# The modulation vector with output channels on partitions: one fused VectorE operation per weight tile

## The chip, the cores and the metric

The kernel runs as one program on one core of a Trainium2 chip. The metric is the device time of one execution in microseconds. Besides TensorE (PE) the core has VectorE (DVE), ScalarE (ACT), GpSimd (POOL) and the sync engine (SP), which issues most DMAs; each takes its instructions in its own order, and semaphores tie them together.

## The reference

Two transformer blocks of width 2048 work on 256 tokens, all in fp32. The first block is modulated by a conditioning vector `c` of 2048 numbers; that modulation is the part that changes:

```python
cond = jax.nn.silu(c)                                   # (1, 2048)
mod = cond @ w_ada[i] + b_ada[i]                        # (2048) x (2048, 12288)
shift1, scale1, gate1, shift2, scale2, gate2 = jnp.split(mod, 6, axis=-1)
h = _rms(x, norm1_w) * (1 + scale1) + shift1            # then in_proj, SSM, attention
x = x + gate1 * mixed
h2 = _rms(x, norm2_w) * (1 + scale2) + shift2           # then the gated FFN
x = x + gate2 * ffn
```

Everything else (projections, a state-space mixer, dilated attention, a second block with neighbourhood, latent and memory attention and a second FFN) is matrix products with 256 rows and small work between them.

## The kernel before, in words

Every weight comes in tiles of 1 MB (128 partitions by 2048 floats) through a ring of six buffers `r`; SP issues the loads in the order of one list `W`. A tile of a matrix product is split into two fp32r parts, halves of 1024 columns at a time: ACT copies it to `h` (line 207) and DVE computes the rest `l = r - h` (line 208). TensorE then makes three products per tile (lines 221, 222 and 226, the last of them on `l`).

The 96 tiles of `w_ada` (kind "a" in the list) are strewn between those (function `mixed`): 32 tiles for shift1 and scale1 among the first products, 48 for gate1, shift2 and scale2 among the next, 16 for gate2 in the first FFN. They don't go to TensorE. A tile holds 2 x 128 input channels by 1024 output channels, input channels on partitions, and the generator `s_ada` gives it to DVE: two operations (line 950) `acc += r[:, j] * cond[j]`, with `cond` one number per partition. Eight tiles make one half of one of the six vectors (1024 outputs), whose sum over partitions still has to be taken. `ada_end` does that on TensorE: for shift and scale eight products with a column of ones (line 969, each in two passes, so 16 matmul records), which put output channels on partitions, and a small DVE operation (973 or 975) that fetches them; for a gate two products of 512 columns with a matrix of ones (line 960), which spread the row over all partitions, and two ACT copies (962). `acc` has two buffers; POOL clears one (945) and ACT loads the bias into its first row (946).

The order on every engine is the order in which the Python generators emit: `Flow.run` goes through the list, hands an "a" tile to `s_ada`, splits a "w" tile, sends the tile before it to the products, and then lets every waiting task take one step. No scheduler changes it later.

Of the kernel before, what the change touches and what calls it, by code (L numbers as in the profile page):

```python
# [10 lines left out]
F32 = mybir.dt.float32  # L11
F32R = mybir.dt.float32r
AF = mybir.ActivationFunctionType
OP = mybir.AluOpType
# [9 lines left out]
SP = 4  # L24
# [20 lines left out]


def _vec_layout():
    names = (("c", 16), ("norm1_w", 16), ("norm2_w", 16), ("mem_norm_2", 16),
             ("ln_mix_2", 16), ("ln_mem_2", 16), ("ln_ffn_2", 16), ("q_norm_w", 1),
             ("k_norm_w", 1), ("q_norm_2", 4), ("kv_norm_2", 2), ("na_out_norm_2", 8),  # L50
             ("mla_out_norm_2", 8))
    out, o = {}, 0
    for n, k in names:
        out[n] = (o, k)
        o += k
    return out, o
# [28 lines left out]
def layout(inp):  # L85
    g = {k: np.asarray(v) for k, v in inp.items()}
    perm = _token_order()
    a = {}
    a["x"] = np.ascontiguousarray(g["x"][0][perm].reshape(2, 128, 4, 512).transpose(2, 1, 0, 3))
    a["mem"] = np.ascontiguousarray(g["mem_2"][0].reshape(2, 128, 4, 512).transpose(2, 1, 0, 3))  # L90
    a["vec"] = np.concatenate([_pp(g[n].reshape(-1)) for n in VEC], axis=1)
    a["b_ada"] = np.ascontiguousarray(g["b_ada"].reshape(1, 12288))
    a["fnorm"] = np.ascontiguousarray(g["final_norm_2"].reshape(1, 2048))
    a["bias1"], a["rope"] = _constants()
    a["w_ada"] = np.ascontiguousarray(
        g["w_ada"][0].reshape(8, 2, 128, 12, 1024).transpose(3, 0, 2, 1, 4))
    a["w_in"] = _wtiles(g["w_in"][0])
    a["w_glu"] = _wtiles(g["ssm_w_glu"][0])
    a["w_out"] = _wtiles(g["w_out"][0])
    for s, d in (("w_ffn_gate", "wg1"), ("w_ffn_up", "wu1"), ("w_ffn_down", "wd1"),  # L100
                 ("w_gate_2", "wg2"), ("w_up_2", "wu2"), ("w_down_2", "wd2"),
                 ("w_out_2", "w_out2"), ("w_xq_2", "w_xq"), ("w_xk_2", "w_xk"),
                 ("w_xv_2", "w_xv"), ("w_xo_2", "w_xo")):
        a[d] = _wtiles(g[s][0])
    w2 = g["w_in_2"][0]
    a["w_qkv2"] = _wtiles(np.ascontiguousarray(w2[:, :3072]))
    a["w_cq"] = _wtiles(np.ascontiguousarray(w2[:, 3072:3584]))
    a["w_ckv"] = _wtiles(np.ascontiguousarray(w2[:, 3584:]), 320)
    uq = g["w_uq_2"][0].reshape(512, 8, 192)
    a["w_uq"] = _wtiles(np.concatenate([uq[:, :, :128].reshape(512, 1024),  # L110
                                        uq[:, :, 128:].reshape(512, 512)], axis=1))
    kv = g["w_ukv_2"][0].reshape(256, 8, 2, 128).transpose(0, 2, 1, 3).reshape(2, 128, 2, 2, 512)
    a["w_ukv"] = np.ascontiguousarray(kv.transpose(2, 1, 3, 0, 4)).reshape(2, 1, 128, 4, 512)
    rpb = g["na_rpb_2"][0]
    t = perm.reshape(2, 128)
    r, c = t // 64, t % 64
    rk, ck = perm // 64, perm % 64
    start = np.clip(c - 8, 0, 48)
    ok = (ck[None, None] >= start[..., None]) & (ck[None, None] < start[..., None] + 16)
    dr = rk[None, None] - r[..., None] + 7  # L120
    dc = np.clip(ck[None, None] - c[..., None] + 15, 0, 30)
    nb = np.where(ok[None], rpb[:, dr, dc], np.float32(-1e30))
    a["nabias"] = np.ascontiguousarray(nb.transpose(0, 2, 1, 3).reshape(8, 128, 512))

    def state(v):
        return v.reshape(32, 2, 64).transpose(1, 2, 0).reshape(128, 32)

    ldt = np.repeat(g["ssm_log_dt"][0].reshape(64, 1), 64, axis=1)
    dd = np.tile(g["ssm_d"][0].reshape(32, 32).T, (4, 1))
    a["ssm_p"] = np.ascontiguousarray(  # L130
        np.stack([state(g["ssm_a_re"][0]), state(g["ssm_a_im"][0]), state(ldt), dd], 1))
    bc = []
    for i, n in enumerate(("ssm_b_re", "ssm_b_im", "ssm_c_re", "ssm_c_im")):
        v = g[n][0]
        if i >= 2:
            v = v.transpose(0, 2, 1)
        bc.append(v.reshape(NSEC, SP, 2, 64, 16).transpose(0, 2, 3, 1, 4).reshape(NSEC, 128, SP, 16))
    a["ssm_bc"] = np.ascontiguousarray(np.stack(bc, 2))
    return a
# [299 lines left out]
class Ssm:  # L439
# [272 lines left out]
    def run(self, s, u4, ytok):  # L712

        k, nc = self.k, self.k.nc
        V, G = nc.vector, nc.gpsimd
        xt, C, T, E = self.sec.pop(s)
        unit = lambda: k.unit((128, 2, SP, 64))
        S = k.pm((128, 2, SP, 64))
# [4 lines left out]
        a, b, c = unit(), unit(), unit()  # L723
# [19 lines left out]
                nc.tensor.matmul(ps[:, q, 1:64], C[:, i, q, 1:5].rearrange("p a b -> p (a b)"),  # L743
                                 a[:, i, q, 0:63], start=False, stop=i == 1)
        self.done = s
        y4 = self.pool.tile([128, SP, 64], F32, name=k.nm("y"), tag="y4", bufs=2)
        nc.scalar.activation(y4, ps, AF.Gelu_apprx_tanh)
        yield
        for h in range(2):
# [6 lines left out]
def build(ctx, tc, A, out):  # L756
# [20 lines left out]
    def v(n, i, m=1):  # L777
        return vec[:, VEC[n][0] + i:VEC[n][0] + i + m]
# [110 lines left out]
            x[g][t] = unit()  # L889
            S.dma_start(x[g][t], A["x"][g][:, t])  # L890

    cond = k.const([128, 16], "cond")
    S.activation(cond, v("c", 0, 16), AF.Silu)
    wqk = k.const([128, 1], "wqk")
    V.tensor_tensor(wqk, v("q_norm_w", 0), v("k_norm_w", 0), op=OP.mult)
    V.tensor_scalar(wqk, wqk, 128.0 ** -0.5, None, op0=OP.mult)
# [38 lines left out]
        return done  # L935


    md = {i: k.const([128, 16], f"mod{i}") for i in (0, 1, 3, 4)}
    gate = {2: [], 5: []}

    def s_ada():

        for h in (2, 0, 3, 1) + ADA + (10, 11):
            acc = k.up.tile([128, 1024], F32, name=k.nm("acc"), tag="acc", bufs=2)
            G.memset(acc, 0.0)
            S.dma_start(acc[0:1], A["b_ada"][:, h * 1024:h * 1024 + 1024])
            for kb in range(8):
                r = yield
                for j in range(2):
                    V.scalar_tensor_tensor(acc, r[:, j], cond[:, 2 * kb + j:2 * kb + j + 1], acc,  # L950
                                           op0=OP.mult, op1=OP.add)
            fl.add(ada_end(h // 2, h % 2, acc))
        yield

    def ada_end(i, half, acc):
        if i in gate:
            yield
            for j in range(2):
                ps = k.pm()
                PE.matmul(ps, k.ones, acc[:, 512 * j:512 * j + 512], start=True, stop=True)  # L960
                row = (unit if i == 2 else unit2)()
                S.activation(row, ps, AF.Copy)
                gate[i].append(row)
            return
        yield
        yield
        ps = k.pm((128, 8))
        for j in range(8):
            PE.matmul(ps[:, j:j + 1], acc[:, j * 128:(j + 1) * 128], k.ones[:, 0:1], start=True, stop=True)
        o = md[i][:, 8 * half:8 * half + 8]  # L970
        if i in (1, 4):
            w = v("norm1_w" if i == 1 else "norm2_w", 8 * half, 8)
            V.scalar_tensor_tensor(o, ps, 1.0, w, op0=OP.add, op1=OP.mult)
        else:
            V.tensor_copy(o, ps)
        got.add((i, half))
        yield

# [660 lines left out]
```

## Time and profile before

| | |
|---|---|
| time, median of 3 runs | 2726.45 us (2726.13 to 2727.95) |
| the profiled execution | 2723.84 us, of it the span from first to last instruction 2721.8 us |
| TensorE busy | 2628.7 us (97% of the span) |
| VectorE busy | 1691.5 us (62%) |
| ScalarE busy | 1258.8 us (46%) |
| GpSimd busy | 103.2 us (4%) |
| DMA | 577.97 MB, mean 212 GB/s |
| DVE line 950 (the modulation) | 192 operations, 245.8 us, from 31.0 to 862.6 us |

A busy TensorE is not one at its peak, since its matmuls overlap and their ends are modelled; so stretches are compared by what waits for what. The work of the modulation lies in the first 884 us only. From 884 to 2650 us nothing of it is left.

### The profile page before, as it was taken

How to read it: one execution, taken by the hardware profiler on the slowest of the kernel's cores; microseconds unless marked ns; L12 is line 12 of the kernel's file. 1: busy time of each engine (PE TensorE's matmuls, PEld its weight loads, DVE VectorE, ACT ScalarE, POOL GpSimd, SP SyncE). 2: the span in 40 equal slices, each digit the busy share in tenths (PEclk: the TensorE clock that was granted, in tenths of full speed). 3: DMA queues.
4: the chain of work that ended last, by engine and by line, in shares of the span. 5: the costliest groups of instructions: out<-in, count | busy, mean ns of one | idle time of the engine just before them, and what ended most of it. 6: DMA issues, size and time to landing. Idle time of an engine off the chain costs nothing.

```text
span 2721.8 us, 31521 instructions
## 1 busy us (share of the span) xinstructions
PE 2628.7 (97%) x12272; PEld 2184.9 (80%) x12272; DVE 1691.5 (62%) x2128; ACT 1258.8 (46%) x1786; POOL 103.2 (4%) x115
## 2 busy tenths in 40 slices
PE   8989988988999999999999999999999999999998
PEld 6778777776788888888888878888888888888887
DVE  7996999979676554555465454655554544455444
ACT  5464545553544444433445555554544433443433
POOL 3000000100000000000000021100000000000001
PEclk9999999999999999999999999999999999999999
DMA  8988766667576555555545434455455555555552
GB/s 337 346 302 321 278 239 227 239 228 305 221 284 267 190 185 198 187 199 186 194 164 191 178 132 147 178 189 183 170 213 194 191 191 191 196 186 185 186 200 94
DMA packets 90029, 577.97 MB, mean 212 GB/s; under 512 B 9996, under 2 KB 12428, under 8 KB 22680
## 3 DMA queue, kind: packets, MB, share of 16 engines
q1 hardware_dynamic: 80928, 561.61, 55.5%
q10 hardware_dynamic: 8952, 14.34, 1.6%
q8 instruction: 96, 1.57, 0.2%
q14 instruction: 53, 0.43, 0.0%
HBM read 569.63 MB, written 6.29 MB: 212 GB/s over the span
## 4 chain that ended last, share of the span: by engine, by line
PE 79%; DVE 11%; issue 7%; ACT 2%; DMA 1%; POOL 0%; SPq 0%; ACTq 0%; DVEq 0%; POOLq 0%
PE g L226 25%; PE g L221 24%; PE g L222 24%; DVE l L208 3%; DVE acc L950 2%; PE m L238 2%; DVE v L627 1%; ACT h L207 0%; PE m L342 0%; DVE u L732 0%; PE m L1488 0%; PE m L1475 0%; DVE C L635 0%; PE m L240 0%; PE m L329 0%
## 5 line engine op out<-in xcount | busy, mean ns | idle before, releaser
L208 DVE TENSOR_TENSOR l<-r,h 128x1024 fp32r<-128x1024 f32 x866 | 1028.2, 1222 | 562.5 <-ACT h L207 554.9
L221 PE MATMUL g<-h,u 128*128 128x512 f32 x3424 | 1353.0, 395 | 9.2 <-ACT h L207 6.2
L222 PE MATMUL g<-h,u 128*128 128x512 f32 x3424 | 1337.8, 391 | 0.0
L207 ACT ACTIVATE h<-r 128x1024 fp32r<-128x1024 f32 x866 | 884.6, 1056 | 634.7 <-PE g L222 596.6
L226 PE MATMUL g<-l,u 128*128 128x512 f32 x3424 | 922.1, 391 | 39.9 <-DVE l L208 39.7
L226 PEld LDWEIGHTS g<-l,u 128*128 128x128 f32 x3424 | 642.5, 189 | 185.2 <-DVE l L208 52.4
L221 PEld LDWEIGHTS g<-h,u 128*128 128x128 f32 x3424 | 648.0, 189 | 144.8 <-ACT h L207 10.3
L222 PEld LDWEIGHTS g<-h,u 128*128 128x128 f32 x3424 | 647.8, 189 | 132.3 <-issue 1.0
L950 DVE SCALAR_TENSOR_TENSOR acc<-r,cond,acc 128x1024 f32<-128x1024 f32 x192 | 245.8, 1280 | 3.8
L271 ACT ACTIVATE u<-m 128x512 fp32r<-128x512 f32 (+1 forms) x80 | 42.7, 574 | 163.8 <-PE m L238 128.8
L291 ACT ACTIVATE j<-u 128x512 bf16<-128x512 f32 (+2 forms) x92 | 47.3, 514 | 121.1 <-DVE u L1208 34.1
L272 DVE TENSOR_TENSOR u<-m,u 128x512 fp32r<-128x512 f32 (+1 forms) x80 | 50.0, 658 | 85.5 <-ACT u L271 85.4
L274 ACT ACTIVATE u<-m,vec 128x256 fp32r<-128x256 f32 x86 | 38.8, 471 | 74.7 <-PE m L342 32.4
L238 PE MATMUL m<-ident,u 128*128 128x128 f32 x372 | 53.0, 286 | 16.8 <-DMA u<-in_mem_dram 7.8
L275 DVE SCALAR_TENSOR_TENSOR u<-m,vec,u 128x256 fp32r<-128x256 f32 x86 | 40.0, 481 | 45.9 <-ACT u L274 45.9
L238 PEld LDWEIGHTS m<-ident,u 128*128 128x128 f32 x372 | 45.6, 147 | 24.2 <-ACT u L982 6.8
L1255 DVE TENSOR_TENSOR w<-g,w 128x512 f32<-128x512 f32 x24 | 16.5, 687 | 43.4 <-PE g L226 43.4
L1239 DVE SCALAR_TENSOR_TENSOR w<-g,r,w 128x512 f32<-128x512 f32 x22 | 15.5, 747 | 44.4 <-PE g L226 44.4
L299 POOL TENSOR_TENSOR r<-s,mhalf 128x2 f32<-128x2 f32 x5 | 4.4, 889 | 1010.1 <-DVE s L298 1010.1
L1237 DVE TENSOR_TENSOR w<-g,w 128x512 f32<-128x512 f32 x22 | 14.2, 685 | 44.3 <-PE g L226 44.3
L1511 DVE TENSOR_TENSOR u<-g,u 128x512 f32<-128x512 f32 x22 | 14.2, 685 | 44.3 <-PE g L226 44.3
L1231 ACT ACTIVATE w<-g,r 128x512 f32<-128x512 f32 x22 | 13.9, 686 | 52.9 <-PE g L226 52.9
(237 smaller groups left out, 1221.3 us busy)
## 6 DMA issues: line engine op xcount, KB each, us to landing
r<-in_w_ada_dram SPq DMA_DIRECT2D x96, 1024.0 KB, 5.1
r<-in_wg_dram SPq DMA_DIRECT2D x88, 1024.0 KB, 4.8
r<-in_wu_dram SPq DMA_DIRECT2D x88, 1024.0 KB, 4.8
r<-in_wd_dram SPq DMA_DIRECT2D x88, 1024.0 KB, 4.8
r<-in_w_in_dram SPq DMA_DIRECT2D x32, 1024.0 KB, 5.8
r<-in_w_out_dram SPq DMA_DIRECT2D x32, 1024.0 KB, 5.2
r<-in_w_qkv_dram SPq DMA_DIRECT2D x24, 1024.0 KB, 4.8
r<-in_w_xk_dram SPq DMA_DIRECT2D x16, 1024.0 KB, 9.1
```

Of the source, the lines that this page charges most:

```text
L207: nc.scalar.activation(h, r, AF.Copy)
L208: (nc.gpsimd if shared else nc.vector).tensor_tensor(l, r, h.bitcast(F32), op=OP.subtract)
L221: nc.tensor.matmul(ps[t][:, :n], al[:, s], h[:, k], start=first and k == 0, stop=False)
L222: nc.tensor.matmul(ps[t][:, :n], ah[:, s], h[:, k], start=False, stop=False)
L226: nc.tensor.matmul(ps[t][:, :n], ah[:, s], l[:, k], start=False, stop=last and k == len(acts) - 1)
L238: self.nc.tensor.transpose(o, i, self.ident)
L271: nc.scalar.activation(h, ps, AF.Copy)
L272: nc.vector.tensor_tensor(l, ps, h.bitcast(F32), op=OP.subtract)
L274: nc.scalar.activation(h, ps, AF.Copy, scale=w)
L275: nc.vector.scalar_tensor_tensor(l, ps, w, h.bitcast(F32), op0=OP.mult, op1=OP.subtract)
L291: self.nc.scalar.activation(j[:, :n], src, AF.Square, accum_out=acc)
L950: V.scalar_tensor_tensor(acc, r[:, j], cond[:, 2 * kb + j:2 * kb + j + 1], acc, op0=OP.mult, op1=OP.add)
```

## The change

`w_ada` is laid out the other way round: a tile holds 128 output channels (on partitions) by all 2048 input channels (along the row). `cond` becomes a full tile of 128 x 2048, the same row in every partition, loaded by a broadcasting DMA of 1 MB and put through Silu by ACT. One `tensor_tensor_reduce` per tile multiplies the tile by `cond` (writing the product back into the tile) and gives the row sum, started from the bias, as one column of `md`. The bias comes with the other small vectors. Shift and scale need no TensorE product any more. A gate, wanted as a row on all partitions, is built from its column: four ACT copies of the identity, scaled by the column, make a block-diagonal tile `d` of 128 x 512, and the product with ones spreads it. `acc`, its clearing and its bias loads are gone. For room, the tile `y4` of the state-space mixer has one buffer instead of two, and a scratch size for dynamic DMA is set.

```diff
@@ _vec_layout, layout
-    names = (("c", 16), ("norm1_w", 16), ...
+    names = (("norm1_w", 16), ...
-             ("mla_out_norm_2", 8))
+             ("mla_out_norm_2", 8), ("b_ada", 96))
-    a["b_ada"] = np.ascontiguousarray(g["b_ada"].reshape(1, 12288))
+    a["c"] = np.ascontiguousarray(g["c"].reshape(1, 2048))
     a["w_ada"] = np.ascontiguousarray(
-        g["w_ada"][0].reshape(8, 2, 128, 12, 1024).transpose(3, 0, 2, 1, 4))
+        g["w_ada"][0].reshape(2048, 12, 8, 128).transpose(1, 2, 3, 0))
@@ Ssm.run
-        y4 = self.pool.tile([128, SP, 64], F32, name=k.nm("y"), tag="y4", bufs=2)
+        y4 = self.pool.tile([128, SP, 64], F32, name=k.nm("y"), tag="y4", bufs=1)
@@ build
-    cond = k.const([128, 16], "cond")
-    S.activation(cond, v("c", 0, 16), AF.Silu)
+    cond = k.const([128, 2048], "cond")
+    S.dma_start(cond, A["c"].to_broadcast([128, 2048]))
+    S.activation(cond, cond, AF.Silu)
@@ s_ada, ada_end
-    md = {i: k.const([128, 16], f"mod{i}") for i in (0, 1, 3, 4)}
+    md = {i: k.const([128, 16], f"mod{i}") for i in range(6)}
         for h in (2, 0, 3, 1) + ADA + (10, 11):
-            acc = k.up.tile([128, 1024], F32, name=k.nm("acc"), tag="acc", bufs=2)
-            G.memset(acc, 0.0)
-            S.dma_start(acc[0:1], A["b_ada"][:, h * 1024:h * 1024 + 1024])
-            for kb in range(8):
+            for j in range(8):
                 r = yield
-                for j in range(2):
-                    V.scalar_tensor_tensor(acc, r[:, j], cond[:, 2 * kb + j:2 * kb + j + 1], acc,
-                                           op0=OP.mult, op1=OP.add)
-            fl.add(ada_end(h // 2, h % 2, acc))
+                n = 8 * (h % 2) + j
+                V.tensor_tensor_reduce(r, r, cond, 1.0, v("b_ada", 8 * h + j), OP.mult, OP.add,
+                                       md[h // 2][:, n:n + 1])
+            fl.add(ada_end(h // 2, h % 2))
         if i in gate:
             yield
             for j in range(2):
+                d = (unit if i == 2 else unit2)((128, 4, 128))
+                for c in R4:
+                    n = 8 * half + 4 * j + c
+                    S.activation(d[:, c], k.ident, AF.Copy, scale=md[i][:, n:n + 1])
                 ps = k.pm()
-                PE.matmul(ps, k.ones, acc[:, 512 * j:512 * j + 512], start=True, stop=True)
+                PE.matmul(ps, k.ones, d.rearrange("p a b -> p (a b)"), start=True, stop=True)
                 row = (unit if i == 2 else unit2)()
                 S.activation(row, ps, AF.Copy)
                 gate[i].append(row)
             return
         yield
-        yield
-        ps = k.pm((128, 8))
-        for j in range(8):
-            PE.matmul(ps[:, j:j + 1], acc[:, j * 128:(j + 1) * 128], k.ones[:, 0:1], start=True, stop=True)
-        o = md[i][:, 8 * half:8 * half + 8]
         if i in (1, 4):
-            w = v("norm1_w" if i == 1 else "norm2_w", 8 * half, 8)
-            V.scalar_tensor_tensor(o, ps, 1.0, w, op0=OP.add, op1=OP.mult)
-        else:
-            V.tensor_copy(o, ps)
+            o = md[i][:, 8 * half:8 * half + 8]
+            V.scalar_tensor_tensor(o, o, 1.0, v("norm1_w" if i == 1 else "norm2_w", 8 * half, 8),
+                                   op0=OP.add, op1=OP.mult)
         got.add((i, half))
@@ kernel
-    nc = bacc.Bacc("TRN2", target_bir_lowering=False, num_devices=1)
+    nc = bacc.Bacc("TRN2", target_bir_lowering=False, num_devices=1, dynamic_dma_scratch_size=512)
```

On DVE, around the first tile of the modulation, the order before is this (`r` is the tile, `l` and `h` the parts of a weight tile, `u` and `m` belong to the memory activations):

```order
L275 SCALAR_TENSOR_TENSOR u_347<-m_341,vec,u_346 128x256 x2
L275 SCALAR_TENSOR_TENSOR u_358<-m_352,vec,u_357 128x256 x2
L950 SCALAR_TENSOR_TENSOR acc_180<-r_155,cond,acc_180 128x1024 x2
L208 TENSOR_TENSOR l_370<-r_183,h_369 128x1024
L208 TENSOR_TENSOR l_374<-r_183,h_373 128x1024
```

And this is the same place in the changed kernel:

```order
L275 SCALAR_TENSOR_TENSOR u_347<-m_341,vec,u_346 128x256 x2
L275 SCALAR_TENSOR_TENSOR u_358<-m_352,vec,u_357 128x256 x2
L948 ISA r_158,mod_112<-r_158,cond,vec 128x2048
L948 ISA mod_112 128x1
L208 TENSOR_TENSOR l_369<-r_183,h_368 128x1024
L208 TENSOR_TENSOR l_373<-r_183,h_372 128x1024
```

Nothing moved: in place of two operations of 1024 columns stand one of 2048 columns and a second, one-column instruction that writes the sum to `mod`.

On ACT, at the first half of gate2 in the first FFN, the order before (`w` are tiles of the second pool, `m` is a PSUM tile, `h` the first part of a weight tile):

```order
L207 ACTIVATE h_6553<-r_6438 128x1024
L207 ACTIVATE h_6557<-r_6438 128x1024
L962 ACTIVATE w_6590<-m_6588 128x512
L962 ACTIVATE w_6594<-m_6592 128x512
L207 ACTIVATE h_6604<-r_6476 128x1024
L207 ACTIVATE h_6608<-r_6476 128x1024
```

And in the changed kernel, where line 964 is the copy of a finished row and `mod_116` the column of gate2:

```order
L207 ACTIVATE h_6376<-r_6266 128x1024
L207 ACTIVATE h_6380<-r_6266 128x1024
L960 ACTIVATE w_6411<-ident,mod_116 128x128 x4
L964 ACTIVATE w_6418<-m_6416 128x512
L960 ACTIVATE w_6420<-ident,mod_116 128x128 x4
L964 ACTIVATE w_6427<-m_6425 128x512
L207 ACTIVATE h_6436<-r_6303 128x1024
L207 ACTIVATE h_6440<-r_6303 128x1024
```

The second block-diagonal tile stands behind the copy of the first row, which waits for TensorE's first product; before, TensorE's two products stood side by side with nothing of ACT between them.

## Rows read from the trace of the kernel before

**Rows 1.** The page's first part: busy us, share of the span, instructions.
```profile
PE 2628.7 (97%) x12272; PEld 2184.9 (80%) x12272; DVE 1691.5 (62%) x2128; ACT 1258.8 (46%) x1786; POOL 103.2 (4%) x115
```
**Rows 2.** Windows: length, busy us of PE, PEld, DVE, ACT, POOL; PEclk, DMA share, GB/s.
```profile
5.00:10.00 5.00, 1.99 (x8) 1.54 (x8) 1.84 (x4) 1.78 (x4) 4.92 (x5) 1.00 0.97 357
30.00:204.00 174.00, 157.10 (x724) 126.67 (x723) 165.33 (x290) 90.25 (x140) 10.18 (x10) 0.97 0.88 321
204.00:272.00 68.00, 67.26 (x320) 56.00 (x319) 47.23 (x45) 30.87 (x40) 1.91 (x2) 1.00 0.81 321
272.00:544.00 272.00, 244.89 (x1324) 207.56 (x1323) 260.20 (x484) 139.46 (x294) 16.38 (x14) 0.96 0.65 246
544.00:680.00 136.00, 114.53 (x527) 92.24 (x526) 116.63 (x146) 62.89 (x102) 1.59 (x2) 0.96 0.70 266
748.00:884.00 136.00, 136.00 (x606) 111.45 (x605) 90.80 (x81) 56.55 (x64) 0.00 (x0) 1.00 0.72 275
```
**Rows 3.** Windows of line 950 alone: length, busy us of DVE, PEclk, DMA.
```profile
30.00:204.00 174.00, 63.98 (x50) 0.97 0.88 321
272.00:544.00 272.00, 84.37 (x66) 0.96 0.65 246
544.00:680.00 136.00, 38.38 (x30) 0.96 0.70 266
```
**Rows 4.** DVE groups: line, shapes, count | busy us, mean ns | idle before, releaser.
```profile
L208 DVE TENSOR_TENSOR l<-r,h 128x1024 fp32r<-128x1024 f32 x858 | 1022.1, 1226 | 560.2 <-ACT h L207 554.5 <-DMA r<-in_w_qkv_dram 1.9
L1256 DVE TENSOR_TENSOR u<-u,w 128x512 f32<-128x512 f32 x24 | 16.6, 692 | 0.8
L975 DVE COPY mod<-m 128x8 f32<-128x8 f32 x4 | 0.7, 164 | 6.0 <-PE m L969 5.9
```
**Rows 5.** DVE timeline, 88 to 102 us: start, duration, engine, line, operation, count.
```profile
88.63 2.35 DVE L208 TENSOR_TENSOR l<-r,h 128x1024 fp32r<-128x1024 f32 x2
...
91.33 0.18 DVE L468 TENSOR_TENSOR s<-pr,pi 128x32 f32<-128x32 f32 x1
91.43 0.18 DVE L468 TENSOR_TENSOR s<-pi,pr 128x32 f32<-128x32 f32 x1
...
99.20 2.60 DVE L950 SCALAR_TENSOR_TENSOR acc<-r,cond,acc 128x1024 f32<-128x1024 f32 x2
101.71 1.22 DVE L208 TENSOR_TENSOR l<-r,h 128x1024 fp32r<-128x1024 f32 x1
```
**Rows 6.** ACT timeline, 0 to 14 us; brackets: idle before, releaser.
```profile
2.90 0.22 ACT L893 ACTIVATE cond<-vec 128x16 f32<-128x16 f32 x1 [0.45 <-DMA vec<-in_vec_dram]
...
11.01 2.00 ACT L207 ACTIVATE h<-r 128x1024 fp32r<-128x1024 f32 x2 [1.76 <-DMA u<-in_mem_dram]
...
13.44 0.19 ACT L291 ACTIVATION_READ_ACCUMULATOR j<-u 128x1 f32 x1
13.66 0.63 ACT L291 ACTIVATE j<-u 128x512 bf16<-128x512 f32 x1
```
**Rows 7.** PE timeline, 210 to 213 us, at a half of shift and scale.
```profile
210.83 1.84 PE L969 MATMUL m<-ones,acc 128*128 128x1 f32 x16
212.53 0.49 PE L221 MATMUL g<-h,u 128*128 128x512 f32 x1
```
**Rows 8.** Timeline of PE and ACT at gate2 (784 us), and ACT at 365 us.
```profile
784.29 1.88 PE L960 MATMUL m<-acc,ones 128*128 128x512 f32 x4
785.35 0.60 ACT L962 ACTIVATE w<-m 128x512 f32<-128x512 f32 x1 [6.14 <-PE m L960]
...
365.53 2.45 ACT L1066 ACTIVATE u<-u,s 128x128 f32<-128x128 f32 x8
```
**Rows 9.** Timeline of ACT and DVE at the mixer's second `y4`, 334 to 346 us.
```profile
334.60 0.38 ACT L747 ACTIVATE y<-m 128x256 f32<-128x256 f32 x1 [1.98 <-PE m L743]
...
338.27 0.50 DVE L750 STREAM_TRANSPOSE u<-y 128x128 f32<-128x128 f32 x2
...
343.82 2.35 DVE L208 TENSOR_TENSOR l<-r,h 128x1024 fp32r<-128x1024 f32 x2
```

More of the change, by code (lines that the diff above doesn't have):

```diff
@@ L47, in _vec_layout @@
 def _vec_layout():
-    names = (("c", 16), ("norm1_w", 16), ("norm2_w", 16), ("mem_norm_2", 16),
+    names = (("norm1_w", 16), ("norm2_w", 16), ("mem_norm_2", 16),
              ("ln_mix_2", 16), ("ln_mem_2", 16), ("ln_ffn_2", 16), ("q_norm_w", 1),
              ("k_norm_w", 1), ("q_norm_2", 4), ("kv_norm_2", 2), ("na_out_norm_2", 8),
-             ("mla_out_norm_2", 8))
+             ("mla_out_norm_2", 8), ("b_ada", 96))
     out, o = {}, 0
@@ L943, in s_ada, with ada_end @@
         for h in (2, 0, 3, 1) + ADA + (10, 11):
-            acc = k.up.tile([128, 1024], F32, name=k.nm("acc"), tag="acc", bufs=2)
-            G.memset(acc, 0.0)
-            S.dma_start(acc[0:1], A["b_ada"][:, h * 1024:h * 1024 + 1024])
-            for kb in range(8):
+            for j in range(8):
                 r = yield
-                for j in range(2):
-                    V.scalar_tensor_tensor(acc, r[:, j], cond[:, 2 * kb + j:2 * kb + j + 1], acc,
-                                           op0=OP.mult, op1=OP.add)
-            fl.add(ada_end(h // 2, h % 2, acc))
+                n = 8 * (h % 2) + j
+                V.tensor_tensor_reduce(r, r, cond, 1.0, v("b_ada", 8 * h + j), OP.mult, OP.add,
+                                       md[h // 2][:, n:n + 1])
+            fl.add(ada_end(h // 2, h % 2))
         yield
-    def ada_end(i, half, acc):
+    def ada_end(i, half):
         if i in gate:
```

## The prediction

> **What bounds the kernel now.** I read the page's busy shares first. TensorE is busy 97% of the span, DVE 62% [rows 1], and over the whole kernel that reads as a TensorE bound. But the modulation lives in the first 884 us only, so I then cut that part into windows [rows 2] and asked in each which engine has no idle time. From 30 to 204 us DVE is busy 165.33 of 174 us (95%), TensorE 157.10. From 272 to 544 us DVE is busy 260.20 of 272 us (96%), TensorE 244.89. In both DVE sets the pace. From 204 to 272 us it is the reverse: TensorE 67.26 of 68, DVE 47.23. From 544 to 680 us neither is full (DVE 116.63, TensorE 114.53 of 136): the two hand the wait to each other. From 748 us on TensorE is busy all the time (136.00 of 136 to 884 us). A DVE saving counts in the first two stretches, a TensorE cost counts after 748 us, and that is how the edits are weighed.
>
> Windows of line 950 alone [rows 3] give the tiles of the modulation in each stretch, two operations a tile: 25 from 30 to 204 us, 33 from 272 to 544, 15 from 544 to 680.
>
> **The tile.** Two dependent operations go. From the start of the pair to the start of what follows is 101.71 - 99.20 = 2.51 us [rows 5]. In their place come one pass over 2048 columns and a one-column instruction that delivers the sum. No row of this kernel shows either. The main pass: 512 more columns of a two-input operation cost 1226 - 692 = 534 ns [rows 4], so 1024 more cost 1.07 us. Two independent ones of 1024 take 2.35 us where one alone takes 1.22 [rows 5], so one follows the other after 1.13 us. Main pass 1.13 + 1.07 = 2.20 us, if it streams at that rate. The delivery: from below 0.10 us, the distance between two small operations (91.33 to 91.43) [rows 5]; from above 0.22 us, what ACT's own accumulator read costs until the next operation starts (13.44 to 13.66) [rows 6]. I take 0.18, nearer the second, since that one is the same kind of step. So a tile costs 2.38 us (2.30 to 2.42) and saves 0.13 us. All tiles of the first two stretches and half of those of the mixed one count: 25 + 33 + 7.5 = 65.5, times 0.13 = 8.5 us less. That is small for 192 operations removed: the number of columns that DVE goes over is the same, and only the fixed part of one operation and the wait between the two dependent ones go.
>
> [...]
>
> **The start.** `cond` was ready at 3.1 us, from a few numbers [rows 6]. Now ACT's queue stands until a 1 MB broadcast has landed and a 2048-column Silu has run, about 2 us by the 2.00 us of two 1024-column copies [rows 6]. DMA is full there already (0.97 busy, 357 GB/s from 5 to 10 us [rows 2]), and the first weight split at 11.01 us waits for a landing [rows 6]. So 1.05 MB more at 357 GB/s puts everything back by 2.9 us, and the Silu is hidden in that same wait. DVE has no slack after 30 us to win it back. I take +3.0 (from +1, if the broadcast runs beside the rest, to +6, if it lands late and the Silu shows).
>
> **The products that go.** Eight groups of line 969 leave TensorE. One costs 212.53 - 210.83 = 1.70 us there [rows 7]. Two groups lie between 204 and 272 us, where TensorE sets the pace: -3.4 us. The other six lie where DVE does, and I count 0 for them (bounds 0 and -10). The DVE operations that fetched the result shrink by four copies of 0.16 us [rows 4]: -0.7. The 5.9 us that DVE waited before these copies [rows 4] lie mostly in the TensorE-bound stretch and bring nothing more. POOL's clearing and ACT's bias loads were on engines with room (POOL 4% [rows 1]): 0.
>
> **The gates.** Here the change adds a wait on the path. Before, the two products of a gate half ran side by side in 1.88 us [rows 8]. Now the second needs a block-diagonal tile whose four ACT copies stand behind the copy of the first row, which waits for the first product. TensorE, in order, stands meanwhile. From the row's 785.35 start 0.60 us for the row [rows 8], then four scaled copies of 128 columns at 2.45/8 = 0.31 us, the last with its tail: 1.3 us [rows 8]; with a hand-over of 0.1 us TensorE goes on near 787.3 instead of 785.2, 2.1 us late. The first block-diagonal tile is free: ACT idled 6.14 us before that point [rows 8]. The two halves of gate2 lie where TensorE is always busy: 2 x 2.1 = +4.2 us. The weight splits queued behind on ACT move by the same 2.1 us, not more, so TensorE finds them as before. The two halves of gate1 lie near 542 and 610 us, where waits are shared: between 0 and 2.1 each, I take 1.5, +3.0.
>
> **One `y4`.** The mixer's next Gelu now waits until DVE has transposed the last one. Only one pair is close: the Gelu of 334.60 precedes the transposes of 338.27 [rows 9]. ACT would stand 4 us, with weight splits behind the Gelu; DVE needs them at 343.82, after operations it has anyway, so the cover is there. +0.5 (0 to 4).
>
> **Sum** against the profiled execution of 2723.84 us (span 2721.8 and 2 us around it): +3.0 - 8.5 - 3.4 - 0.7 + 4.2 + 3.0 + 0.5 = -1.9 us. That execution is 2.6 us under the median of the runs; I take the difference to the median, 2726.45 - 1.9 = 2724.5 us.
>
> **Rivals.** Without the tile, the terms add to +6.6 us; so the tile decides, and the sum is zero at a tile of 2.41 us.
>
> 1. The sum is delivered late. The pair of dependent operations takes 2.51 us where two independent ones would take 2 x 1.13 = 2.26 [rows 5]: about 0.25 us of waiting for a result. If the delivering instruction waits for the main pass like that, a tile is 2.38 + 0.25 = 2.63 us, 0.12 over before: +7.9 instead of -8.5, in all +14.5, 2741 us. It decides from 2.51 us a tile on, where the sum is +6.6. For it: an instruction that does nothing but deliver has nothing to overlap with. Against it: ACT's read takes 0.22 us in all [rows 6].
>
> 2. The fused operation streams at half rate: 2.13 us more for a tile, 4.5 us. Then 73 tiles between 30 and 680 us (DVE has no room there) pay 2.0 us each, +146, and the rest of the sum +6.6: about 2879 us. DVE would still have room from 204 to 272 us and after 748 us. Against it: line 950, with two fp32 inputs from SBUF, ran at the full rate [rows 5], but it had no sum along the row. [...]
>
> 3. TensorE's relief pays in the DVE stretches as well. There TensorE is also busy over 90%, and DVE's splits wait on buffers that TensorE gives back. If the six groups count at 1.70 us, -10: 2714 us. Against it: TensorE mostly waits for `l` there, so that what it saves is waited for.
>
> **Chances.** A measurement of this kernel can tell a change from none at about 0.2%, 5.5 us. Forecast 55%, with its own range 2718 to 2731; late delivery 17%; half rate 8%; relief 20%. Faster by over 0.2%: nearly all of the relief and a third of the forecast's spread, 0.36. Within 0.2%: most of the forecast and little of the others, 0.37. Slower: late delivery, half rate and the forecast's upper end, 0.27. The range runs from the relief with the better tile, 2711, to late delivery, 2742; the half rate stays outside.
>
> **What would show it.** In the changed profile, the main operation's mean: near 2.3 us the pass is right, near 4.4 rival 2 holds. The distance from its start to the start of the next `l`: 2.38, or over 2.51 (rival 1). ACT's first split near 14 us instead of 11.01. TensorE idle about 2 us between the two products of each half of gate2. DVE busy from 272 to 544 us falling by about 4 us, with the stretch shorter by as much. The prediction is wrong if TensorE's stretches after 884 us change in length, since nothing of the change reaches there.

## The result, and the profile after

The changed kernel takes 2710.7 us (median of 4 runs, 2709.33 to 2711.92), the kernel before, beside it, 2726.29 us (4 runs, 2724.61 to 2727.95): ratio 0.9945, interval 0.9934 to 0.9957. It is 0.55% faster. The profiled execution took 2711.92 us, 11.9 less than that of before. The sign of the sum was right, its size (1.9 us) not; 2710.7 lies at the lower end of the range, 2711 (the measured ratio on the prediction's 2726.45 us gives 2711.5).

The page of the changed kernel, which answers to [rows 1] and [rows 4] (busy us, share, instructions; then operations' count, busy us, mean ns, idle before):

```profile
span 2710.1 us, 31194 instructions
PE 2616.3 (97%) x12144; PEld 2171.3 (80%) x12144; DVE 1670.5 (62%) x2124; ACT 1269.8 (47%) x1818; POOL 98.6 (4%) x103
L948 DVE CUSTOM_DVE_ANT_0 r<-r,cond,vec 128x2048 f32<-128x2048 f32 x96 | 224.5, 2343 | 0.2
```

The fused operation runs 2343 ns, and DVE's busy time falls by only 21 us, under 1% of the span. Its timeline around a tile answers to [rows 5] (start, duration):

```profile
86.05 2.34 DVE L948 CUSTOM_DVE_ANT_0 r<-r,cond,vec 128x2048 f32<-128x2048 f32 x1
88.32 0.08 DVE L948 DVE_READ_ACCUMULATOR2_ANT mod<- 128x1 f32 x1
88.32 2.35 DVE L208 TENSOR_TENSOR l<-r,h 128x1024 fp32r<-128x1024 f32 x2
...
98.64 2.34 DVE L948 CUSTOM_DVE_ANT_0 r<-r,cond,vec 128x2048 f32<-128x2048 f32 x1
100.91 0.08 DVE L948 DVE_READ_ACCUMULATOR2_ANT mod<- 128x1 f32 x1
100.91 1.22 DVE L208 TENSOR_TENSOR l<-r,h 128x1024 fp32r<-128x1024 f32 x1
```

The instruction that delivers the sum (0.08 us) starts at the same moment as the next `l` (88.32 and 100.91 us): it costs nothing on the path. From tile start to the next `l` are 100.91 - 98.64 = 2.27 us, where it was 2.51.

The windows of the changed kernel answer to [rows 2] (length, busy us of PE, PEld, DVE, ACT, POOL; granted clock, DMA share, GB/s):

```profile
30.00:204.00 174.00, 155.08 (x696) 123.41 (x695) 161.61 (x293) 90.97 (x142) 11.49 (x7) 0.97 0.88 324
272.00:544.00 272.00, 246.06 (x1292) 207.13 (x1290) 256.90 (x488) 140.52 (x296) 17.66 (x10) 0.95 0.67 254
748.00:884.00 136.00, 132.30 (x587) 107.84 (x587) 83.73 (x79) 60.96 (x79) 0.00 (x0) 1.00 0.69 257
```

From 748 to 884 us TensorE is no longer always busy: 3.70 us are missing, all of it at gate2, whose first half is this (engine, line; brackets: idle before, releaser), beside [rows 8]:

```profile
771.41 1.02 PE L962 MATMUL m<-w,ones 128*128 128x512 f32 x2
772.47 0.60 ACT L964 ACTIVATE w<-m 128x512 f32<-128x512 f32 x1 [4.98 <-PE m L962]
772.96 1.27 ACT L960 ACTIVATE w<-ident,mod 128x128 f32<-128x128 f32 x4
774.28 1.12 PE L962 MATMUL m<-w,ones 128*128 128x512 f32 x2 [1.85 <-ACT w L960]
```

TensorE's second product waits 1.85 us for the four scaled copies, which wait for the copy of the first row.

Where the time went is read by lining up the same operation in two timelines. The 866 `l` operations of line 208 keep their order in the kernels below; the starts (us) of some of them:

| `l` number | before | changed | c_two | a_gates | d_oneproduct |
|---|---|---|---|---|---|
| 1 | 12.10 | 13.95 | 13.10 | 13.08 | 12.39 |
| 49 | 179.06 | 175.38 | 180.41 | 174.56 | 179.40 |
| 55 | 204.05 | 203.92 | 205.40 | 202.16 | 204.75 |
| 79 | 280.92 | 275.39 | 276.82 | 273.07 | 277.76 |
| 133 | 530.05 | 519.93 | 527.42 | 517.98 | 527.52 |
| 181 | 722.65 | 709.77 | 719.97 | 705.13 | 719.10 |
| 205 | 794.21 | 783.41 | 795.27 | 776.64 | 790.64 |
| 235 | 878.41 | 869.71 | 881.57 | 860.83 | 874.85 |
| 277 | 990.95 | 982.18 | 994.03 | 973.29 | 987.38 |
| 866 | 2703.30 | 2692.36 | 2704.19 | 2686.70 | 2698.08 |

The changed kernel starts 1.85 us late, is 3.68 early at 179 us and 12.9 early at 723 us, gives 4.2 back by 878 us at the two halves of gate2, and ends 10.9 early.

### The profile page after: what moved, and what is told of

Read it like the earlier page. It is cut to its first block, busy times and chain, and to the rows that moved or that the text cites. A ratio compares the mean times of both kernels' runs of the same rounds, so it can differ in the third digit from the quotient of the medians.

```text
span 2710.1 us, 31194 instructions
## 1 busy us (share of the span) xinstructions
PE 2616.3 (97%) x12144; PEld 2171.3 (80%) x12144; DVE 1670.5 (62%) x2124; ACT 1269.8 (47%) x1818; POOL 98.6 (4%) x103
## 4 chain that ended last, share of the span: by engine, by line
PE 79%; DVE 15%; ACT 2%; issue 2%; DMA 1%; POOL 0%; ACTq 0%; DVEq 0%; POOLq 0%
PE g L226 24%; PE g L221 24%; PE g L222 24%; DVE l L208 4%; DVE r L948 4%; PE m L238 2%; DVE v L627 1%; ACT h L207 1%; DVE C L635 0%; PE m L342 0%; PE m L1484 0%; PE m L1471 0%; DVE u L732 0%; PE m L240 0%; PE m L226 0%
## 5 line engine op out<-in xcount | busy, mean ns | idle before, releaser
L948 DVE CUSTOM_DVE_ANT_0 r<-r,cond,vec 128x2048 f32<-128x2048 f32 x96 | 224.5, 2343 | 0.2
```

The lines of the kernel that those rows point to most:

```text
L948: V.tensor_tensor_reduce(r, r, cond, 1.0, v("b_ada", 8 * h + j), OP.mult, OP.add, md[h // 2][:, n:n + 1])
```

## The experiments

**The gates without their wait (a_gates).** Both block-diagonal tiles first, then both products, then both row copies.

```diff
+            ds, pss = [], []
             for j in range(2):
                 d = ...                       # four scaled copies
+                ds.append(d)
+            for d in ds:
                 ps = k.pm()
                 PE.matmul(ps, k.ones, d...)
+                pss.append(ps)
+            for ps in pss:
                 row = ...
```

> The changed kernel, with the gates' work in another order: both block-diagonal tiles first, then both products, then both row copies. Theory: the serial wait between the two products (ACT's row copy and four scaled copies) costs 2.2 us in each gate half. Then the wait of the second product goes, the two halves of gate2 (TensorE-bound stretch) give 4.4 us back and those of gate1 1 to 3.5 us more: 5.5 to 8 us under the changed kernel's 2710.7, ratio to the kernel before 0.991 to 0.9925. Rival: the wait only moves (the weight splits behind the ACT copies come later and TensorE waits for them): under 1.5 us, ratio 0.994.

Measured: 2706.17 us (5 runs, 2704.98 to 2706.72), ratio to before 0.9931 (0.9917 to 0.9944). The same place in its timeline:

```profile
766.77 1.88 PE L965 MATMUL m<-w,ones 128*128 128x512 f32 x4
767.83 0.60 ACT L969 ACTIVATE w<-m 128x512 f32<-128x512 f32 x1 [3.81 <-PE m L965]
768.69 0.60 ACT L969 ACTIVATE w<-m 128x512 f32<-128x512 f32 x1 [0.26 <-PE m L965]
```

The products are side by side again. By the table a_gates gains on the changed kernel 2.13 us from number 181 to 205 and 2.11 from 205 to 235, the two halves of gate2, and 2.69 from 133 to 181, over gate1. So the gates cost 6.9 us in the changed kernel by these two profiles. The end shows 5.7 of it at the last `l` (this execution lost time near 1550 us, below) and 4.5 between the medians, short of the 5.5 to 8 us expected, and the ratio misses 0.991 to 0.9925; but the rival's "under 1.5 us" is further off.

**The tile alone, undone in size (c_two).** Two chained fused operations of 1024 columns instead of one of 2048; all else as in the changed kernel.

```diff
-                V.tensor_tensor_reduce(r, r, cond, 1.0, v("b_ada", 8 * h + j), OP.mult, OP.add,
-                                       md[h // 2][:, n:n + 1])
+                o = md[h // 2][:, n:n + 1]
+                V.tensor_tensor_reduce(r[:, 0:1024], r[:, 0:1024], cond[:, 0:1024], 1.0,
+                                       v("b_ada", 8 * h + j), OP.mult, OP.add, o)
+                V.tensor_tensor_reduce(r[:, 1024:2048], r[:, 1024:2048], cond[:, 1024:2048], 1.0,
+                                       o, OP.mult, OP.add, o)
```

> The changed kernel, each tile summed by two chained fused operations of 1024 columns in place of one of 2048 (the second starts from the first one's sum). Theory: the change won by the price of a tile on DVE, 2.27 us instead of 2.51; with two chained operations a tile costs 2.5 to 2.7 us, the distance to the kernel before stops growing from 12 to 180 us (it grew by 5.5 us), and the end is 8 to 16 us over the changed kernel: ratio 0.9975 to 1.0005. Rival: the gain came from the products that left TensorE and the time of a tile matters little: under 4 us over, ratio up to 0.996.

Measured: 2726.1 us (11 runs, 2723.77 to 2728.84), ratio to before 1.0004 (0.9995 to 1.0012). A tile of it on DVE:

```profile
87.44 1.28 DVE L949 CUSTOM_DVE_ANT_0 r<-r,cond,vec 128x1024 f32<-128x1024 f32 x1
88.64 0.09 DVE L949 DVE_READ_ACCUMULATOR2_ANT mod<- 128x1 f32 x1
88.76 1.28 DVE L951 CUSTOM_DVE_ANT_0 r<-r,cond,mod 128x1024 f32<-128x1024 f32 x1
89.97 0.08 DVE L951 DVE_READ_ACCUMULATOR2_ANT mod<- 128x1 f32 x1
89.97 2.35 DVE L208 TENSOR_TENSOR l<-r,h 128x1024 fp32r<-128x1024 f32 x2
```

The tile takes 89.97 - 87.44 = 2.53 us, what it took before, and the whole gain is gone: at the last `l` c_two is 11.83 us behind the changed kernel. With 2.53 us a tile the rest of the change sums to nothing. And the tile's 0.26 us reach the end about 11.83 / 0.26 = 46 times in this pair of executions, not 96. The medians lie further apart, 15.4 us (13.4 from the second measurement of the changed kernel, below), which is 52 to 59 times. The table says where: 5.88 us from number 1 to 49 (all of the 22 tiles there), 3.55 given back from 49 to 55, 6.06 from 79 to 133 (30 tiles), 2.71 from 133 to 181 (19 tiles), 1.66 from 181 to 205.

The last of these is not the tile. At gate2 TensorE stands 1.85 us in both kernels, but behind that the granted clock differs (same columns as above; first the changed kernel, then c_two, each behind its second product):

```profile
775.00:780.00 5.00, 5.00 (x22) 3.95 (x22) 2.52 (x4) 2.49 (x3) 0.00 (x0) 1.00 0.64 210
```
```profile
785.00:790.00 5.00, 5.00 (x15) 3.49 (x14) 2.71 (x4) 2.49 (x3) 0.00 (x0) 0.68 0.60 210
```

s_none and h_memset, whose tiles are those of the changed kernel, lose the same there (number 181 to 205 takes 75.28 and 75.27 us, in c_two 75.30, in the changed kernel 73.64) at 0.66 and 0.68. So in these three executions this half of gate2 took 1.63 to 1.66 us beyond its wait of 2.1; that the wait brings the lower clock is not shown. Without this, and from number 1 on (c_two starts 0.85 us earlier), the pair shows 11.0 us, 42 times.

What was given back between 179 and 204 us stands in two windows, first of the changed kernel, then of c_two (columns as above):

```profile
174.00:180.00 6.00, 3.46 (x13) 2.56 (x12) 5.67 (x9) 2.96 (x6) 2.01 (x1) 0.70 0.95 329
180.00:186.00 6.00, 6.00 (x22) 4.75 (x21) 4.69 (x7) 5.18 (x9) 0.00 (x0) 0.73 0.64 203
```
```profile
174.00:180.00 6.00, 4.54 (x19) 3.11 (x17) 5.90 (x14) 0.26 (x1) 1.66 (x1) 1.00 0.92 365
180.00:186.00 6.00, 5.20 (x26) 4.34 (x27) 5.87 (x13) 5.36 (x12) 0.00 (x0) 1.00 0.86 329
```

In the changed kernel TensorE's granted clock falls to 0.70 and 0.73 there (0.50 from 178 to 182 us), and in c_two it is 1.00 in both windows. DVE's saving arrived at the norm while TensorE's granted clock was that low. In the second execution of the changed kernel (after_again) and in y_two, h_memset, s_none and b_cond number 49 to 55 takes 27.4 to 27.8 us (28.54 here, 24.99 in c_two and before), at a clock of 0.72 to 0.83 from 174 to 180 us, and in g_best, with 1.00 there, 26.15; so 2.4 to 2.8 us of the 3.55 are lost again in each of these five. That the clock is their cause is argued from these rows, not isolated.

**Half the tile (f_half).** The fused operation over the first 1024 columns only.

```diff
-                V.tensor_tensor_reduce(r, r, cond, 1.0, ...
+                V.tensor_tensor_reduce(r[:, 0:1024], r[:, 0:1024], cond[:, 0:1024], 1.0, ...
```

> The changed kernel with the fused operation over the first 1024 of the 2048 columns only; it leaves out half of every sum. A tile costs DVE 1.2 us in place of 2.27. Theory: DVE sets the pace from 30 to 204 us only by a little; TensorE, busy 155 of 174 us there, takes over soon: the stretch from 12 to 175 us shortens by 10 to 17 us and not by 24 tiles times 1.07 = 26 us, and the end comes 20 to 40 us earlier, ratio 0.980 to 0.987. Rival: DVE alone sets the pace in its stretches: 26 us there and over 60 us at the end, ratio under 0.973; or a tile's time is lost later in TensorE's stretches: under 12 us.

Measured: 2655.89 us (4 runs, 2653.22 to 2656.84), ratio 0.974 (0.9727 to 0.9753). A tile of it, and the window from 30 us to the start of number 49:

```profile
81.85 1.28 DVE L948 CUSTOM_DVE_ANT_0 r<-r,cond,vec 128x1024 f32<-128x1024 f32 x1
83.05 0.08 DVE L948 DVE_READ_ACCUMULATOR2_ANT mod<- 128x1 f32 x1
```
```profile
30.00:154.00 124.00, 123.76 (x580) 102.42 (x579) 117.64 (x261) 69.59 (x107) 7.65 (x7) 1.00 1.00 400
```

A tile is 1.07 us shorter, 102.7 us over 96 tiles; the last `l` starts 59.0 us earlier than in the changed kernel, 57%; the medians differ by 54.8 us, 53%. From number 1 to 49 it gains 20.3 us, between the 10 to 17 expected and the rival's 26; the end came earlier than the 20 to 40 us expected, nearer to the rival. In this stretch TensorE is busy 123.76 of 124 us now and the DMA share is 1.00, where the changed kernel has 155.08 of 174 us and 0.88 from 30 to 204. So the bound has changed over there, to TensorE or to DMA; the two are not separated.

**The products alone (d_oneproduct).** The kernel before with one product of eight columns where it had eight of one.

```diff
-        for j in range(8):
-            PE.matmul(ps[:, j:j + 1], acc[:, j * 128:(j + 1) * 128], k.ones[:, 0:1], start=True, stop=True)
+        PE.matmul(ps, acc[:, 0:128], k.ones[:, 0:8], start=True, stop=True)
```

> The kernel before, with one product of 8 columns in place of the eight of one column in each half of shift and scale; it leaves out seven eighths of these sums. Theory: TensorE's relief of some 1.5 us a half counts only where TensorE is on the path: the two halves near 210 and 256 us and the last one at 675 us, together 3 to 5.5 us, ratio 0.998 to 0.999. Rival: all eight halves count (12 us, ratio 0.9956), so that the products explain most of the change; or none does (ratio 1.000).

Measured: 2719.78 us (11 runs, 2716.92 to 2721.52), ratio 0.9981 (0.9972 to 0.999). Against before the table shows 0.3 late at number 1, nothing gained to 55, 3.86 from 55 to 79, 0.41 more up to 277 (3.57 ahead), and 1.65 after that, where nothing was changed. The two groups in the TensorE-bound stretch bring 3.9 us. Of the six others nothing clear is seen: 0.6 us are lost from 79 to 133, and 1.0 gained from 133 to 181, where the last group stands (674.72 us) and the granted clock from 680 to 695 us is 0.89 instead of 0.77, which is not separated from it.

**The start (b_cond, s_none).** First the broadcast behind the first group of memory activations and the wide Silu behind the third (a one-column Silu, `warm`, stays at the start).

```diff
+    warm = k.const([128, 1], "warm")
+    S.activation(warm, v("q_norm_w", 0), AF.Silu)
-    S.dma_start(cond, A["c"].to_broadcast([128, 2048]))
-    S.activation(cond, cond, AF.Silu)
@@ s_mem
+            if g == 0:
+                S.dma_start(cond, A["c"].to_broadcast([128, 2048]))
+            if g == 2:
+                S.activation(cond, cond, AF.Silu)
```

> The changed kernel, with the broadcast of c issued from ACT after the first activations and its Silu run behind the third ones (Silu's table is loaded at the start as before). Theory: the late start of the changed kernel (first weight split of DVE 1.84 us later) comes from ACT's queue standing behind the broadcast; the split is back within 0.4 us of the kernel before and the 1.8 us reach the end: ratio 0.9938. Rival: the 1 MB itself, on full DMA queues, delays the weights whenever it is sent: the first split moves by less than 0.7 us, or the loss returns some tiles later; ratio 0.9945.

Measured: 2712.27 us (5 runs, 2710.11 to 2713.8), ratio 0.9954 (0.9941 to 0.9966): no gain. Its first `l` starts at 11.89, 2.06 earlier than in the changed kernel; at number 7 only 0.24 is left (34.86 against 35.10). ACT's timeline of b_cond says why:

```profile
22.58 0.47 ACT L274 ACTIVATE u<-m,vec 128x256 fp32r<-128x256 f32 x1 [0.58 <-DVE u L275]
22.95 1.91 ACT L915 ACTIVATE cond<-cond 128x2048 f32<-128x2048 f32 x1
24.76 1.99 ACT L207 ACTIVATE h<-r 128x1024 fp32r<-128x1024 f32 x2
```

The Silu's 1.91 us stand ahead of a weight split here as well. The expected 0.9938 was missed; the rival, a loss that returns some tiles later, is nearer, with the Silu as what brings it. Then `cond` was filled by POOL, with neither load nor Silu:

```diff
-    S.dma_start(cond, A["c"].to_broadcast([128, 2048]))
-    S.activation(cond, cond, AF.Silu)
+    G.memset(cond, 0.5)
```

> The changed kernel with `cond` filled by POOL with 0.5 instead of loaded and put through Silu (it leaves out the load of c and the Silu): neither the 1 MB broadcast nor ACT's 1.91 us Silu stands at the start. Theory: the changed kernel's loss at the start is these two and nothing else, so the first weight split starts at 11.0 us or before, as in the kernel before (changed kernel 12.87, 11.77 in its second profile), and the whole kernel is 1 to 2 us faster, 2709 to 2710 us. Rival: the loss is a shift of the start that comes with every execution, or with another part of the change; then the first split stays at 11.8 to 12.9 us and the time at 2711 us.

Measured: 2708.95 us (5 runs, 2707.26 to 2709.78), ratio 0.9936 (0.9924 to 0.9948). ACT's first split, in the changed kernel and then here:

```profile
8.25 1.91 ACT L894 ACTIVATE cond<-cond 128x2048 f32<-128x2048 f32 x1 [5.31 <-DMA cond<-in_c_dram]
...
12.87 1.99 ACT L207 ACTIVATE h<-r 128x1024 fp32r<-128x1024 f32 x2
```
```profile
10.32 1.99 ACT L207 ACTIVATE h<-r 128x1024 fp32r<-128x1024 f32 x2
```

The first split comes 2.55 us earlier, and the time is 1.7 us below the changed kernel's 2710.7 (3.8 below the 2712.72 of its second measurement, next). At the start the theory holds: load and Silu together cost 2.55 us against this execution and 1.45 against the second (11.77 instead of 12.87). At the end 1.7 to 3.8 us fit it, but the intervals of the ratios overlap.

**The control (after_again).** The changed kernel once more, unaltered.

> The changed kernel once more, beside the next ones on the same chip: ratio 0.9945 to the kernel before, within 0.001.

Measured: 2712.72 us (5 runs, 2707.25 to 2713.88), ratio 0.9946 (0.9933 to 0.9958). Its start, beside the one above:

```profile
7.16 1.91 ACT L894 ACTIVATE cond<-cond 128x2048 f32<-128x2048 f32 x1 [4.22 <-DMA cond<-in_c_dram]
...
11.77 1.99 ACT L207 ACTIVATE h<-r 128x1024 fp32r<-128x1024 f32 x2
```

The landing of the broadcast alone varies by 1.1 us between two executions of one kernel. A term of the start is known to about 1 us, no better.

**One `y4` or two (y_two).**

```diff
-        y4 = self.pool.tile([128, SP, 64], F32, name=k.nm("y"), tag="y4", bufs=1)
+        y4 = self.pool.tile([128, SP, 64], F32, name=k.nm("y"), tag="y4", bufs=2)
```

> The changed kernel with two buffers for `y4` again. Theory: one buffer costs nothing, since DVE has finished the transposes before the next Gelu wants the buffer or ACT's stand is covered: 2711 us, within 1 us of the changed kernel. Rival (the upper bound of the prediction): ACT stands up to 4 us once and DVE, which sets the pace there, waits for it: 2707 us.

Measured: 2711.69 us (5 runs, 2707.55 to 2711.86), ratio 0.9943 (0.9931 to 0.9956): one buffer costs nothing that can be told.

**A POOL operation beside DVE's scaled copies (h_memset).** In the kernel before, a POOL clearing of `acc` ran beside the second norm's two scaled identities. The changed kernel has no such clearing; here four smaller ones were put there.

```diff
+        zz = pool2[0].tile([128, 256], F32, name="zz", tag="zz", bufs=1)
+        for _ in range(4):
+            G.memset(zz, 0.0)
```

> The changed kernel with four POOL memsets of 128 x 256 put right behind the reciprocal root of the second norm, where the kernel before had one of 128 x 1024 (0.95 us). Theory: DVE's two scaled copies of the identity, 0.48 us together in the changed kernel and 1.01 us in the kernel before, were slowed by that memset: they take about 1 us again, and what follows moves by 0.5 us. Rival: their time has another reason and stays at 0.48 us.

One profiled run, 2712.56 us. The two copies in before, in the changed kernel, and here:

```profile
685.55 0.95 POOL L945 MEMSET acc<- 128x1024 f32 x1
685.64 1.01 DVE L1217 TENSOR_SCALAR w<-ident,r 128x128 f32<-128x128 f32 x2 [0.81 <-POOL r L299]
```
```profile
674.20 0.48 DVE L1213 TENSOR_SCALAR w<-ident,r 128x128 f32<-128x128 f32 x2 [0.81 <-POOL r L299]
```
```profile
672.88 1.42 POOL L1213 MEMSET zz<- 128x256 f32 x4
672.97 0.68 DVE L1216 TENSOR_SCALAR w<-ident,r 128x128 f32<-128x128 f32 x2 [0.81 <-POOL r L299]
```

0.48 us alone, 0.68 beside the short clearings, 1.01 beside the long one. So a clearing beside them slows the copies, by 0.20 us here; that the one of before accounts for all of its 0.53 us is likely, not shown. The prediction priced this edit at nothing.

**A better version (g_best), and two more (g_late, g_rows).** The gates of a_gates, and Silu on 128x16 values, written to DRAM as a row and broadcast from there.

```diff
+    c16 = k.const([128, 16], "c16")
+    S.dma_start(c16, A["c"].rearrange("o (p a) -> (o p) a", p=128))
+    S.activation(c16, c16, AF.Silu)
+    crow = k.dp.tile([1, 2048], F32, name="crow")
+    S.dma_start(crow.rearrange("o (p a) -> (o p) a", p=128), c16)
@@ s_mem
+            if g == 0:
+                S.dma_start(cond, crow.to_broadcast([128, 2048]))
```

> The changed kernel with the gates' work in the other order (both block-diagonal tiles, both products, both row copies) and with the Silu taken on 128 x 16 numbers before the broadcast: they go to DRAM and come back as the 128 x 2048 tile, issued behind ACT's first activations. Theory: what the changed kernel lost at the start was the 2 us of the wide Silu in ACT's queue (run b_cond gave the first split 2.05 us back, and lost 1.81 of it four splits later, where it had put the Silu); without it the start is that of the kernel before and stays so to 179 us, 1.5 to 2 us, and the gates give 4.3 us or more: ratio 0.9915 to 0.993. Rival: the 1 MB itself costs DMA time where weights wait: the first gain is gone by 60 us, ratio 0.993 to 0.994.

Measured: 2705.39 us (5 runs, 2704.77 to 2707.53), ratio to before 0.9925 (0.9911 to 0.9938). It beats both kernels, but by the gates alone; the start did not improve. ACT's timeline:

```profile
4.96 0.34 ACTq L897 DMA_DIRECT2D crow<-c  x1
...
12.46 0.34 ACTq L916 DMA_DIRECT2D cond<-crow  x1
12.85 2.00 ACT L207 ACTIVATE h<-r 128x1024 fp32r<-128x1024 f32 x2 [3.69 <-DMA crow<-c]
```

The second load is issued from ACT's own queue and waits there until the row has landed in DRAM, and ACT's first split stands behind it for 3.69 us. A wait of 5.31 us was exchanged for another. So the issue was moved behind the second group (`if g == 1`), in g_late, and in g_rows `c16` is also held as 16 x 128.

> The small Silu and the gates of the last version, with the broadcast of the finished row issued from ACT's queue behind the second group of memory activations instead of the first. In the last version ACT stood 3.69 us before its first split, behind that issue, until the row had landed. Theory: that stand goes, the first split comes at 11.0 us instead of 12.85, nothing wide stands on ACT later, and the time is 1 to 2 us below the 2705.4 us of the last version: 2703.5 to 2704.5. Rival: the 1 MB takes its share of the DMA engines wherever it stands and is given back by the first tile, at 33 us: no gain, 2705.4.

> The same order as the version before it (small Silu, row written to DRAM, broadcast issued behind the second group of memory activations, gates reordered), but c is held as 16 partitions by 128 values, so that the row goes to DRAM in 16 pieces of 512 B instead of 128 pieces of 64 B, and the Silu passes over 128 columns instead of 16. Theory: the order sets the time, so 2702 to 2704 us, first split at 10.0 to 11.0 us. Rival: the wider Silu or the other write stands on ACT's way again: 2705 us.

Measured: 2702.49 us (5 runs, ratio 0.9914, 0.99 to 0.9927) and 2702.08 us (5 runs, 0.9914, 0.99 to 0.9927). The first split of g_rows comes at 9.35 us, that of g_late at 10.22:

```profile
10.22 1.99 ACT L207 ACTIVATE h<-r 128x1024 fp32r<-128x1024 f32 x2
...
15.97 0.33 ACTq L916 DMA_DIRECT2D cond<-crow  x1
```

But these two cannot be offered as versions. Besides the broadcast, their edit changes a second `if g == 2`, in `done_uq` of the second block, which picks the queries that get the rotary embedding:

```diff
@@ done_uq
             o = tok(ps, lat["rq"])
-            if g == 2:
+            if g == 1:
```

So they compute something else, and near 1550 us, where this place runs, the order of the operations is another than in g_best. They are read for the first 900 us alone, and there the rival is nearer: the first `l` is 2.64 us earlier than in g_best (11.30 against 13.94), number 181 only 0.34 (704.78 against 705.12). The shorter total comes from after 990 us.

## Why the prediction was right or wrong

**The tile: mis-sized, and this is the step that failed.** The prediction took 2.20 us for the pass and 0.18 us for the delivery. The pass is 2.27 us to the next start, the delivery 0: its price was taken from ACT's accumulator read [rows 6], but DVE's next operation starts with the read, not behind it. A tile saves 0.24 us, not 0.13. By the prediction's own count of 65.5 tiles that would be 15.7 us; c_two shows 11.0 to 11.8 in its profile and 15.4 between the medians, so 42 to 59 tiles pay, and the count was too high. The two errors go in opposite directions; the term was 2.5 to 6.9 us too small. The other part of the miss is in the rest of the sum, which had +6.6 us where nothing is found.

That the time landed at the edge of the range is luck. Its lower end was set by the relief of TensorE with the better tile, and d_oneproduct rules this relief out; by the prediction's own terms that corner is also 2714.3 - 65.5 x 0.08 = 2709 us, not 2711.

In the trace the 2.27 us are the pass alone, and the delivering instruction (0.08 us) adds nothing. A chained operation pays more: in c_two the second one starts 88.76 - 88.64 = 0.12 us after the read begins.

**The rest of the change: +6.6 forecast, about 0 measured** (c_two, 1.0004 of before, 0.9995 to 1.0012; 0.9 us late at the last `l`). By terms:

- The start: +3.0 forecast, +1.85 in the profiled execution at the first `l`, 0.75 in after_again's (12.85 against 12.10). The first split comes at 12.87 and 11.77 us, not near 14. The prediction had hidden the Silu in the landing; in the trace it stands behind it, and s_none shows both together worth 1.45 to 2.55 us.
- The products: -3.4 forecast; d_oneproduct shows -3.9 from number 55 to 79 and nothing clear elsewhere, so the count of two groups was right. From before to c_two the same stretch gains 5.45. Of the 1.6 us between these, the eighth of the products that d_oneproduct keeps is about 0.4; the rest has no run of its own. A candidate is DVE's wait before the small copies [rows 4], counted as nothing: it is 5.71 us at 258.07 us before and 4.15 in d_oneproduct, where TensorE then waits 2.72 and 2.71 us for `l` near 280 us; c_two has no such copy and waits 0.23.
- gate2: +4.2 forecast, 4.24 measured (a_gates), and 1.65 more in the executions whose clock falls behind the wait. gate1: +3.0 forecast, 2.7 measured. Here the mechanism and the size held. But from 133 to 181, where gate1 lies, c_two is no slower than before (192.55 and 192.60 us), so about as much was gained there, and what gained it was not separated.
- `y4`: +0.5 forecast, nothing found (y_two).
- A gain not forecast: POOL's clearing beside the second norm's copies, 0.53 us in the rows, 0.20 of it by h_memset.
- Time after 884 us, where the prediction said that a change would prove it wrong: number 277 to 866 takes 1712.35 us before and 1710.18 after. The windows of the span in between, of before, of the changed kernel and of a_gates:

```profile
1540.00:1600.00 60.00, 54.99 (x263) 45.53 (x262) 29.10 (x39) 37.04 (x70) 11.67 (x13) 0.97 0.41 141
```
```profile
1540.00:1600.00 60.00, 55.02 (x267) 45.44 (x266) 31.39 (x42) 36.91 (x71) 13.55 (x15) 1.00 0.38 134
```
```profile
1500.00:1540.00 40.00, 38.01 (x174) 31.40 (x173) 15.32 (x13) 22.13 (x29) 0.00 (x0) 0.96 0.49 168
1540.00:1600.00 60.00, 57.00 (x269) 47.54 (x268) 30.83 (x44) 32.83 (x69) 13.66 (x16) 0.97 0.37 134
```

The mean granted clock there is 0.97 before and 1.00 after, which for 60 us is an estimated 1.8 us. a_gates, faster as a whole, has 0.96 and 0.97 and loses instead; after_again, the same kernel as the changed one, has 0.97 from 1540 to 1600 us and ends 0.8 us behind it. From 277 to 866 after_again takes 1712.24 us, as long as before. So these 2.2 us of the profiled difference belong, as far as the rows show, to the execution and not to the change.

**The rivals.** Late delivery fell: the next operation starts with the read (both at 100.91 us). Half rate, for which no row of the kernel before spoke, fell: 2343 ns for 2048 columns, where two operations of 1024 took 2.51 us. TensorE's relief (-10 us beyond the two groups) fell with d_oneproduct, 4.9 us below before in all.

**What stays open.** Why DVE's saving pays 42 to 59 times of 96: the rows show the granted clock at 174 to 186 us (0.70 and 0.73) and TensorE at 246.06 of 272 us in the second stretch, and f_half shows a similar share (53 to 57%; c_two 44 to 62%) for a saving four times as large, so it looks like a property of these stretches and not of this edit; which wait takes each lost part was not separated.

## What to carry to other kernels

When a reduction along the row replaces an accumulation over partitions, count the dependent pairs that go: the delivery of the sum (0.08 us) was free here, and one operation of 2048 columns beat two of 1024 by 0.26 us. Here, where one engine was 95% and the next 90% busy in the stretches that counted, about half of a saving on the first reached the end (44 to 62%). Look at every place where a product waits for a copy that waits for an earlier product: emitting all operands first, then all products, was worth 4.5 us here at the end and 6.9 where it stands.

## What the runs showed of the hardware beyond that

DVE's read of its accumulator takes 0.08 us in the row and no time on the path when the next operation doesn't need the sum, as in the rows above (100.91 us). Of ACT's reads at the start of before, one took 0.22 us until the next operation (13.44 to 13.66 us) and one 0.09 (14.20 to 14.29 us). Two DVE copies of 128x128 took 0.48 us alone, 0.68 beside four short POOL clearings and 1.01 beside one of 0.95 us. Behind the same 1.85 us in which TensorE stood, the granted clock was 1.00 in two executions of the changed kernel and 0.66 to 0.68 over the next 5 us in c_two, s_none and h_memset. A write of 8 KB from 128 partitions to DRAM, 64 bytes each, took 7.5 us from its issue at 4.96 us to the load behind it at 12.46 us; the same bytes in 16 pieces of 512 (g_rows) landed 5.8 us after their issue.
